# Down projection of layer 1 as seven Strassen products per pair of chunks, in two passes, on one Trainium2 core

## The chip, the cores and the metric

The kernel is one program on one core of a Trainium2 chip. The metric is the time of one execution on the device in microseconds, the median of three runs.

## The reference, cut to what matters

The model is an encoder of two layers over 1024 tokens of 1024 channels. Each layer ends in a SwiGLU feed-forward part of width 2816, and the last step is a norm:

```python
def swiglu_ffn(h, w_gate, w_up, w_down):
    return (jax.nn.silu(h @ w_gate) * (h @ w_up)) @ w_down
...
        h = rmsnorm(x, norm_ffn_g[layer])
        x = x + swiglu_ffn(h, ffn_w_gate[layer], ffn_w_up[layer], ffn_w_down[layer])
    return rmsnorm(x, final_g)
```

The change concerns the last product, `@ w_down`, for layer 1, what comes right before it (the activations silu(gate) * up) and right behind it (residual sum and final norm).

## The kernel before, in words

Everything lies transposed: channels on the 128 partitions, tokens along the free axis. The residual is 8 tiles `xs[k]` of 128 channels by 1024 tokens. The hidden width is 22 chunks of 128. All products are in fp32 accuracy from three matmuls of the shorter type fp32r: an operand is split into a high part (a cast on ACT, L87) and the rest (a subtraction on DVE, L88), and `mm3` (L98) adds high x high, high x low and low x high in one PSUM bank.

The program is recorded in Python order; a scheduler then sets the order on each engine and places the waits, and each engine goes through its own list in order. Buffers come from pools of a fixed number: 28 `big` tiles (one holds a 512-token operand with both of its parts, or one residual tile), 10 `w` tiles, 3 `raw` tiles for loads, 6 `half` tiles, and two each of `cv` and `pr`. An allocation waits until a tile of its pool is free.

Gate and up (`gate_up_first` L608, `gate_up_all` L684). The feed-forward part already takes its first two products as Strassen's seven in Winograd's form: two chunks of the hidden width, two halves of the channels and two halves of the tokens (`HALVES`, 512 each). `prep` (L626) forms the weight sums for a pair `p` (11 pairs) one unit of products ahead, `gate_up_rest` (L655) does the products, `fin` (L647) takes silu or the product with up and sends the activation to DRAM (`a_dram`) from GpSimd's queue (L653). GpSimd does nothing else in this stage.

Down (`down`, L737). The first half of the tokens comes whole, then the second. For each half the hidden chunks go in groups of 8, 7 and 7 (`GROUPS`). `load_a` (L708) loads the activations of a group back and splits them, `load_w` (L108) loads and splits the weights of a group for one of the 8 output chunks, and `down_one` (L721) accumulates the chunks of a group in one PSUM bank and adds the bank to the residual on DVE (L726). That is 22 x 8 x 3 matmuls of 512 columns for the first half and, because the second half is given in two parts of 256 tokens, twice as many of 256 columns for the second. `final` (L876) squares and sums the residual over the channels (L133, L134, a matmul with ones L538), takes the root (L122 to L125), scales (L882) and stores (L884). For the first half it runs behind the products of the second; `run_behind` (L728) hands out its instructions. For the last 256 tokens it is the tail of the program.

## Time and profile before

| what | value |
|---|---|
| the three runs | 1743.06, 1745.55 and 4281.53 us, median 1745.55 |
| span of the profiled execution | 1740.6 us, first to last instruction |
| matmuls, TensorE busy | 8318 in 1682.0 us |
| DVE, ACT, GpSimd (POOL) busy | 1245.9, 692.9, 276.0 us |
| granted TensorE clock | 0.991 on average |
| moved by DMA | 238.66 MB, 137 GB/s |

The third run is an outlier of the machine and takes no part in what follows. The time of a run holds some start and end around the span: the median lies 4.95 us over the span of the profiled execution, whose own time is not listed apart. A row of the profile gives the line of the code, the engine, the operation, output and inputs with their form, the count, then the busy time, the mean length of one and the idle time before it with what ended it. PEld is TensorE's loading of weights, which runs beside its matmuls; SP is the engine whose queue issues most loads.

### The profile page before, as it was taken

How to read it: one execution, taken by the hardware profiler on the slowest of the kernel's cores; microseconds unless marked ns; L12 is line 12 of the kernel's file. 1: busy time of each engine (PE TensorE's matmuls, PEld its weight loads, DVE VectorE, ACT ScalarE, POOL GpSimd, SP SyncE). 2: the span in 40 equal slices, each digit the busy share in tenths (PEclk: the TensorE clock that was granted, in tenths of full speed). 3: DMA queues.
4: the chain of work that ended last, by engine and by line, in shares of the span. 5: the costliest groups of instructions: out<-in, count | busy, mean ns of one | idle time of the engine just before them, and what ended most of it. 6: DMA issues, size and time to landing. Idle time of an engine off the chain costs nothing.

```text
span 1740.6 us, 22375 instructions
## 1 busy us (share of the span) xinstructions
PE 1682.0 (97%) x8318; PEld 1400.9 (80%) x8318; DVE 1245.9 (72%) x1774; ACT 692.9 (40%) x1062; POOL 276.0 (16%) x300
## 2 busy tenths in 40 slices
PE   6998899999999999999999998999999999999997
PEld 4786777777888888889998886778888888788997
DVE  8699988794577777755559768787777775545546
ACT  5455855464323232233234344553232322334223
POOL 4587764111000000000000001110000000000000
PEclk9999899999999999999999999999999999999999
DMA  5121311545633333355433425646333333644433
GB/s 188 47 97 37 135 61 46 184 142 201 232 131 122 127 109 127 116 167 174 133 109 126 152 85 182 211 163 218 133 122 127 109 127 121 204 144 160 167 122 123
DMA packets 82236, 238.66 MB, mean 137 GB/s; under 512 B 10320, under 2 KB 15696, under 8 KB 82128
## 3 DMA queue, kind: packets, MB, share of 16 engines
q1 hardware_dynamic: 65520, 186.64, 32.6%
q0 software_dynamic: 14304, 47.46, 7.2%
q10 hardware_dynamic: 2304, 3.15, 0.5%
q8 instruction: 65, 1.06, 0.3%
q14 instruction: 43, 0.35, 0.1%
HBM read 190.02 MB, written 47.19 MB: 136 GB/s over the span
## 4 chain that ended last, share of the span: by engine, by line
PE 83%; DVE 11%; DMA 3%; ACT 1%; issue 1%; SPq 0%; DVEq 0%; ACTq 0%
PE ps L100 18%; PE ps L102 18%; PE ps L101 18%; PE lnp L100 10%; PE lnp L102 10%; PE lnp L101 9%; DVE acc L313 2%; DVE acc L134 1%; DMA xin<-in_xT 1%; DMA raw<-in_wd 1%; DVE hl L88 1%; DMA raw<-in_wu 1%; DVE wl L88 1%; DVE ybl L88 0%; PE lnp L538 0%
## 5 line engine op out<-in xcount | busy, mean ns | idle before, releaser
L87 ACT CAST hl<-raw 128x512 fp32r<-128x512 f32 x264 | 161.2, 621 | 426.0 <-DVE raw L636 161.4
L100 PE MATMUL ps<-hl 128*128 128x512 f32 x704 | 277.6, 395 | 3.3 <-ACT s L617 2.8
L102 PE MATMUL ps<-hl 128*128 128x512 f32 x704 | 276.6, 393 | 0.0
L101 PE MATMUL ps<-hl 128*128 128x512 f32 x704 | 276.5, 393 | 0.0
L87 ACT CAST wh<-raw 128x896 fp32r<-128x896 f32 (+2 forms) x139 | 132.5, 953 | 243.5 <-PE ps L101 109.0
L100 PE MATMUL ps<-ahl,wh 128*128 128x256 f32 (+3 forms) x711 | 228.0, 321 | 0.5 <-ACT wh L87 0.5
L102 PE MATMUL ps<-ahl,wl 128*128 128x256 f32 (+3 forms) x711 | 227.7, 320 | 0.5 <-DVE wl L88 0.5
L101 PE MATMUL ps<-ahl,wh 128*128 128x256 f32 (+3 forms) x711 | 227.2, 320 | 0.0
L88 DVE TENSOR_TENSOR hl<-raw,hl 128x512 fp32r<-128x512 f32 x264 | 179.8, 689 | 47.9 <-ACT hl L87 43.3
L100 PE MATMUL lnp<-hl 128*128 128x512 f32 x528 | 210.2, 398 | 0.7 <-ACT s L617 0.7
L102 PE MATMUL lnp<-hl 128*128 128x512 f32 x528 | 208.1, 395 | 0.0
L101 PE MATMUL lnp<-hl 128*128 128x512 f32 x528 | 207.9, 394 | 0.0
L88 DVE TENSOR_TENSOR wl<-raw,wh 128x896 fp32r<-128x896 f32 (+2 forms) x127 | 141.6, 1116 | 48.7 <-ACT wh L87 44.3
L100 PEld LDWEIGHTS ps<-hl 128*128 128x128 f32 x704 | 132.2, 188 | 37.7 <-ACT s L617 6.9
L102 PEld LDWEIGHTS ps<-hl 128*128 128x128 f32 x704 | 132.3, 188 | 30.6
L101 PEld LDWEIGHTS ps<-hl 128*128 128x128 f32 x704 | 132.4, 188 | 29.6
L303 POOL TENSOR_TENSOR cvp<-cvp,pr 128x512 f32<-128x512 f32 x96 | 139.3, 1452 | 82.5 <-ACT pr L302 78.2
L100 PEld LDWEIGHTS ps<-ahl,wh 128*128 128x128 f32 x711 | 134.3, 189 | 11.1 <-ACT wh L87 0.9
L102 PEld LDWEIGHTS ps<-ahl,wl 128*128 128x128 f32 x711 | 134.0, 189 | 10.9 <-DVE wl L88 1.0
L101 PEld LDWEIGHTS ps<-ahl,wh 128*128 128x128 f32 x711 | 134.3, 189 | 10.2 <-issue 0.2
L653 POOL DMA_DIRECT2D a<-g x66 | 35.6, 540 | 576.6 <-DVE g L652 576.6
L100 PEld LDWEIGHTS lnp<-hl 128*128 128x128 f32 x528 | 99.5, 189 | 27.3 <-ACT s L617 4.3
(209 smaller groups left out, 3095.9 us busy)
## 6 DMA issues: line engine op xcount, KB each, us to landing
raw<-in_wg SPq DMA_DIRECT2D x66, 512.0 KB, 3.4
raw<-in_wu SPq DMA_DIRECT2D x66, 512.0 KB, 3.6
raw<-in_wd SPq DMA_DIRECT2D x72, 448.0 KB, 3.3
a<-g POOLq DMA_DIRECT2D x88, 256.0 KB, 3.1
raw<-in_wd SPq DMA_DIRECT2D x32, 512.0 KB, 3.8
p<-s POOLq DMA_DIRECT2D x44, 256.0 KB, 3.2
u<-p SPq DMA_DIRECT2D x44, 256.0 KB, 4.2
raw<-a SPq DMA_DIRECT2D x44, 256.0 KB, 3.3
```

The costliest lines, as they stand in the source:

```text
L87: nc.scalar.copy(hi, src)
L88: (eng or nc.vector).tensor_tensor(out=lo, in0=src, in1=hi.bitcast(F32), op=ALU.subtract)
L100: nc.tensor.matmul(ps, lh, rh, start=start, stop=False, **kw)
L101: nc.tensor.matmul(ps, lh, rl, start=False, stop=False, **kw)
L102: mm = nc.tensor.matmul(ps, ll, rh, start=False, stop=stop, **kw)
L134: TT(out=acc, in0=acc, in1=sq, op=ALU.add)
L303: nc.gpsimd.tensor_tensor(out=a, in0=a, in1=pr, op=ALU.add)
L313: STT(out=acc, in0=src, scalar=wv, in1=acc, op0=ALU.mult, op1=ALU.add)
L653: nc.gpsimd.dma_start(a_dram[layer][m][:, HALVES[t]], dst)
```

## The change

The down projection of layer 1 becomes `down_strassen`. Layer 0 keeps `down`. The left operand A is the weight matrix for a pair of hidden chunks by a pair of output chunks (A11, A12 for the first output chunk, A21, A22 for the second; `j` counts the 4 pairs of output chunks), the right operand B the activations of the pair of hidden chunks by the two halves of the tokens. The seven products in Winograd's form are A11 B11, A12 B21, S1 T1, S2 T2, S3 T3, S4 B22 and A22 T4, with S1 = A21 + A22, S2 = S1 - A11, S3 = A11 - A21, S4 = A12 - S2 and T1 = B12 - B11, T2 = B22 - T1, T3 = B22 - B12, T4 = B21 - T2.

The sums T1 to T4 are made on GpSimd at the end of each pair of the gate and up stage (`combine`) and go to DRAM in place of B12, together with B11, B21 and B22. The sums of weights are made on DVE (`left_a`, `left_b`) from the raw weights, which come in a new layout `wds` and are loaded twice. Pass A takes five of the products, in blocks of 3, 3, 3 and 2 pairs, for each block 4 steps `j`; pass B takes S1 T1 and S4 B22 in blocks of 4, 4 and 3. A finished bank is copied to SBUF by ACT and added to the residual (or to the partial sum `u2`) by GpSimd (`add_pool`), except S2 T2, S4 B22 and, in the last block of pass A, A22 T4, which DVE adds from PSUM. Right operands of the next block are loaded and split during the block before. The final norm takes each half of the tokens whole, the second one as the tail.

```diff
+    PTT = nc.gpsimd.tensor_tensor
...
     def fin(layer, up, dst, src, m, t, tmp=None):
...
-            nc.gpsimd.dma_start(a_dram[layer][m][:, HALVES[t]], dst)
+            store_b(layer, "B%d%d" % (m % 2 + 1, t + 1), m // 2, dst)
+
+    def store_b(layer, name, p, src):
+        if layer == 0:
...
+        elif name != "B12":
+            nc.gpsimd.dma_start(b_dram[name][p], src)
+
+    def combine(p, g):
+        g11 = arena.tile([P, TH], F32, tag="cv", name="g11", bufs=2)
+        nc.sync.dma_start(g11, b_dram["B11"][p])
+        t1, t3 = g11, arena.tile([P, TH], F32, tag="cv", name="t3", bufs=2)
+        t2, t4 = (arena.tile([P, TH], F32, tag="pr", name=n, bufs=2) for n in ("t2", "t4"))
+        PTT(out=t3, in0=g["22"], in1=g["12"], op=ALU.subtract)
+        PTT(out=t1, in0=g["12"], in1=g11, op=ALU.subtract)
+        PTT(out=t2, in0=g["22"], in1=t1, op=ALU.subtract)
+        PTT(out=t4, in0=g["21"], in1=t2, op=ALU.subtract)
+        for name, src in (("T1", t1), ("T2", t2), ("T3", t3), ("T4", t4)):
+            store_b(1, name, p, src)
...
+            if up and layer == 1:
+                combine(p, g)
...
+    def load_b(names, early=False):
+        out = []
+        for n, p in names:
+            if early:
+                raw = half("rawb")
+            else:
+                bturn[0] += 1
+                tag = ("cv", "pr")[bturn[0] % 2]
+                raw = arena.tile([P, TH], F32, tag=tag, name=tag, bufs=2)
+            nc.sync.dma_start(raw, b_dram[n][p])
+            out.append(opnd(raw, big))
+        return out
...
+    def load_quads(j, p0, n):
+        out = []
+        for q in range(2):
+            raw = arena.tile([P, 1024], F32, tag="raw", name="raw", bufs=3)
+            rv = raw.rearrange("p (a c) -> p a c", a=2)[:, :, :n * P]
+            nc.sync.dma_start(rv, wds[j, :, 2 * q:2 * q + 2, p0 * P:(p0 + n) * P])
+            out += [raw[:, :n * P], raw[:, TH:TH + n * P]]
+        return out
...
+    def left_a(j, p0, n):
+        a11, a12, a21, a22 = load_quads(j, p0, n)
+        w = {"A11": wopnd(a11)}
+        s3 = small("s3")[:, :n * P]
+        TT(out=s3, in0=a11, in1=a21, op=ALU.subtract)
+        TT(out=a21, in0=a21, in1=a22, op=ALU.add)
+        TT(out=a21, in0=a21, in1=a11, op=ALU.subtract)
+        w["S2"], w["S3"], w["A12"], w["A22"] = wopnd(a21), wopnd(s3), wopnd(a12), wopnd(a22)
+        return w
+
+    def left_b(j, p0, n):
+        a11, a12, a21, a22 = load_quads(j, p0, n)
+        TT(out=a21, in0=a21, in1=a22, op=ALU.add)
+        TT(out=a11, in0=a21, in1=a11, op=ALU.subtract)
+        TT(out=a12, in0=a12, in1=a11, op=ALU.subtract)
+        return {"S1": wopnd(a21), "S4": wopnd(a12)}
+
+    def down_strassen(layer, blocks_a, blocks_b, gen):
...
+        def add_pool(dst, ps):
+            t = half("u1")
+            nc.scalar.copy(t, ps)
+            PTT(out=dst, in0=dst, in1=t, op=ALU.add)
+
+        def finish_b(bc, s4, b22, x12):
+            product(bc, s4, b22, False, True)
+            TT(out=x12, in0=bc, in1=x12, op=ALU.add)
+
+        for i, (kind, p0, n, j) in enumerate(steps):
...
+            nw = left(i + 1) if i + 1 < len(steps) else None
+            (x11, x12), (x21, x22) = x[j]
+            if kind == "a":
+                ba, bb, bd = single(), single(), single()
+                product(ba, w["A11"], b["B11"], True, True)
+                if u2[j] is None:
+                    u2[j] = arena.tile([P, TH], F32, tag="cvp", name="uu", bufs=4)
+                    nc.scalar.copy(u2[j], ba)
+                else:
+                    add_pool(u2[j], ba)
+                product(bb, w["S2"], b["T2"], True, True)
+                TT(out=u2[j], in0=bb, in1=u2[j], op=ALU.add)
+                product(bd, w["S3"], b["T3"], True, True)
+                add_pool(x22, bd)
+                product(ba, w["A12"], b["B21"], False, True)
+                add_pool(x11, ba)
+                product(bd, w["A22"], b["T4"], False, True)
+                if (p0, n) != blocks_a[-1]:
+                    add_pool(x21, bd)
+                else:
+                    TT(out=x21, in0=bd, in1=x21, op=ALU.add)
+                    TT(out=x21, in0=x21, in1=u2[j], op=ALU.add)
+                    for dst in (x12, x22):
+                        PTT(out=dst, in0=dst, in1=u2[j], op=ALU.add)
+            else:
+                bc = single()
+                product(bc, w["S1"], b["T1"], True, True)
+                add_pool(x22, bc)
+                if late:
+                    finish_b(*late)
+                late = bc, w["S4"], b["B22"], x12
...
+            got += load_b(todo[:k])
...
-    down(1, ([(0, TH)], [(TH, TH + 256), (TH + 256, S)]), final)
+    down_strassen(1, ((0, 3), (3, 3), (6, 3), (9, 2)), ((0, 4), (4, 4), (8, 3)), final)
```

Three places show how the engines' lists change. In the rows below `g` are the activations of a pair, `hl` a split operand (`hl<-raw` a left one, `hl<-rawb`, `hl<-pr` and `hl<-cv` right ones), `uu` the partial sum `u2`, `ps` and `lnp` PSUM banks. Line numbers of the new kernel are those of its own file: there L89 is the subtraction of a split, L664 a store, L672 to L675 `combine`, L883 the add of `add_pool`.

On GpSimd, the end of its list before, from the last pair of the gate and up stage on:

```order
L653 DMA a_18_2345<-g_11518 128x512
L653 DMA a_21_2348<-g_11718 128x512
L653 DMA a_21_2348<-g_11719 128x512
L653 DMA a_20_2347<-g_11720 128x512
L972 UNCONDITIONAL_BRANCH
```

and the same pair now, with the first adds of the down projection:

```order
L664 DMA bB_10_2359<-g_11893 128x512
L664 DMA bB_10_2348<-g_11894 128x512
L672 TENSOR_TENSOR t_12048<-g_11893,g_11895 128x512
L673 TENSOR_TENSOR g_12046<-g_11895,g_12046 128x512
L664 DMA bT_10_2392<-t_12048 128x512
L674 TENSOR_TENSOR t_12049<-g_11893,g_12046 128x512
L664 DMA bT_10_2370<-g_12046 128x512
L675 TENSOR_TENSOR t_12050<-g_11894,t_12049 128x512
L664 DMA bT_10_2381<-t_12049 128x512
L664 DMA bT_10_2403<-t_12050 128x512
L883 TENSOR_TENSOR x_12157<-x_12157,u_12241 128x512
L883 TENSOR_TENSOR x_12159<-x_12159,u_12229 128x512
```

Where GpSimd had nothing left, four sums of the last pair stand now, and 76 adds follow them.

On DVE, the transition: the last unit of the gate and up stage before, in which the splits of the first activations (`ahl`) stand between its sums,

```order
L88 TENSOR_TENSOR ahl<-raw,ahl 128x512 x2
L670 TENSOR_TENSOR u_11824<-lnp,u_11824 128x512
L652 TENSOR_TENSOR g_11718<-u_11824,g_11718 128x512
L88 TENSOR_TENSOR ahl<-raw,ahl 128x512 x2
L677 TENSOR_TENSOR c_11853<-lnp,u_11797 128x512
L652 TENSOR_TENSOR g_11719<-c_11853,g_11719 128x512
L88 TENSOR_TENSOR wl<-raw,wh 128x1024
L681 TENSOR_TENSOR u_11797<-lnp,u_11797 128x512
L652 TENSOR_TENSOR g_11720<-u_11797,g_11720 128x512
```

and now, from the same product of the same unit on:

```order
L694 TENSOR_TENSOR u_11999<-lnp,u_11999 128x512
L89 TENSOR_TENSOR hl<-s_12180,hl 128x384
L656 TENSOR_TENSOR g_11893<-u_11999,g_11893 128x512
L701 TENSOR_TENSOR c_12028<-lnp,u_11972 128x512
L89 TENSOR_TENSOR hl<-raw,hl 128x384
L656 TENSOR_TENSOR g_11894<-c_12028,g_11894 128x512
L705 TENSOR_TENSOR u_11972<-lnp,u_11972 128x512
L89 TENSOR_TENSOR hl<-rawb,hl 128x512
L656 TENSOR_TENSOR g_11895<-u_11972,g_11895 128x512
L89 TENSOR_TENSOR hl<-rawb,hl 128x512 x4
L89 TENSOR_TENSOR hl<-raw,hl 128x384
L89 TENSOR_TENSOR hl<-rawb,hl 128x512 x2
```

The splits between the sums are those of left operands now, and the right operands of the first block come behind the sum L705, which reads the last product of the stage.

On DVE, well inside the down projection: before, one step of the first half of the tokens and the next,

```order
L726 TENSOR_TENSOR x_11880<-ps,x_11880 128x512
L88 TENSOR_TENSOR wl<-raw,wh 128x896
L88 TENSOR_TENSOR ahl<-raw,ahl 128x512
L726 TENSOR_TENSOR x_11882<-lnp,x_11882 128x512
L88 TENSOR_TENSOR wl<-raw,wh 128x896
L88 TENSOR_TENSOR ahl<-raw,ahl 128x512
```

and now, one step in the fourth block of pass A:

```order
L903 TENSOR_TENSOR uu<-ps,uu 128x512
L836 TENSOR_TENSOR s_13544<-raw 128x256
L837 TENSOR_TENSOR raw<-raw 128x256
L838 TENSOR_TENSOR raw<-raw 128x256
L89 TENSOR_TENSOR hl<-raw,hl 128x256
L89 TENSOR_TENSOR hl<-s_13544,hl 128x256
L89 TENSOR_TENSOR hl<-raw,hl 128x256
L912 TENSOR_TENSOR x_12163<-lnp,x_12163 128x512
L89 TENSOR_TENSOR hl<-raw,hl 128x256
L913 TENSOR_TENSOR x_12163<-x_12163,uu 128x512
```

Three instructions for a step of 21 matmuls have become ten for one of 30, and the splits of left operands are five small ones (one stands ahead of these rows) in place of one long one.

More of the change, by code (lines that the diff above doesn't have):

```diff
@@ L43, in trunk @@
 def trunk(ctx: ExitStack, tc: tile.TileContext, xT, vecs, cw, w_in, w_out, fmap, pmap,
-          wg, wu, wd, cen_m, pcnt, dft_h, dft_l, seq_h, seq_l, out):
+          wg, wu, wd, wds, cen_m, pcnt, dft_h, dft_l, seq_h, seq_l, out):
     nc = tc.nc
@@ L527, in single @@
         return bank(("ps", "lnp", "ps")[turn[0] % 3])
-    a_dram = [[dram.tile([P, S], F32, name=f"a{layer}_{f}") for f in range(NF)] for layer in range(2)]
+    a_dram = [[dram.tile([P, S], F32, name=f"a0_{f}") for f in range(NF)]]
+    b_dram = {n: [dram.tile([P, TH], F32, name=f"b{n}_{p}") for p in range(NF // 2)]
+              for n in ("B11", "B21", "B22", "T1", "T2", "T3", "T4")}
     def norm(lo, hi):
@@ L548, in product @@
     def product(ps, w, b, start, stop):
-        for j in range(4):
+        n = len(b)
+        for j in range(n):
             c = j * P
             mm3(ps, (w[:, c:c + P], w[:, TH + c:TH + c + P]), (b[j][:, :TH], b[j][:, TH:]),
-                start and j == 0, stop and j == 3, skip_group_check=not start)
+                start and j == 0, stop and j == n - 1, skip_group_check=not start)
     def h_make(layer, t, bt, hf):
@@ L623, in gate_up_first @@
                 TT(out=g, in0=ps, in1=g, op=ALU.mult)
-        nc.gpsimd.dma_start(a_dram[layer][2 * p][:, HALVES[0]], g)
+        store_b(layer, "B11", p, g)
     def prep(layer, p, wsrc, first):
@@ L770, in down @@
         run_behind(back, 1e9)
+    def load_b(names, early=False):
[10 more added lines that the diff above has]
+        return out
+    bturn = [0]
+    def load_quads(j, p0, n):
[6 more added lines that the diff above has]
+        return out
@@ new lines, in wopnd @@
+    def wopnd(src):
+        t = wtile("hl")
+        n = src.shape[-1]
+        split(t[:, :n], t[:, TH:TH + n], src)
+        return t
+    PASS_A = (("A11", "B11"), ("S2", "T2"), ("S3", "T3"), ("A12", "B21"), ("A22", "T4"))
+    def left_a(j, p0, n):
[7 more added lines that the diff above has]
+        return w
@@ L874, in trunk, with final @@
     gate_up_all(1, b1, NP1)
-    def final(pi, blocks):
-        for lo, hi in blocks:
-            inv = norm(lo, hi)
-            yield 6.0
-            for k in range(KD):
-                o = half("o")[:, :hi - lo]
-                STT(out=o, in0=xs[k][:, lo:hi], scalar=gneg[:, V_FIN + k:V_FIN + k + 1], in1=inv,
-                    op0=ALU.mult, op1=ALU.mult)
-                (nc.sync if k % 2 else nc.scalar).dma_start(out[k][:, lo:hi], o)
-                yield 0.65
-    down(1, ([(0, TH)], [(TH, TH + 256), (TH + 256, S)]), final)
+    def final(t):
+        hs = HALVES[t]
+        inv = norm(hs.start, hs.stop)
+        yield 6.0
+        for k in range(KD):
+            o = half("o")
+            STT(out=o, in0=xs[k][:, hs], scalar=gneg[:, V_FIN + k:V_FIN + k + 1], in1=inv,
+                op0=ALU.mult, op1=ALU.mult)
+            (nc.sync if k % 2 else nc.scalar).dma_start(out[k][:, hs], o)
+            yield 0.65
+    down_strassen(1, ((0, 3), (3, 3), (6, 3), (9, 2)), ((0, 4), (4, 4), (8, 3)), final)
 def _round_f32r(a):
@@ L947 @@
     wd = []
-    for l in range(2):
+    for l in range(1):
         parts, o = [], 0
@@ L954 @@
     a["wd"] = np.stack(wd)
+    a["wds"] = np.ascontiguousarray(
+        f["ffn_w_down"][1].reshape(NF // 2, 2, P, 4, 2, P).transpose(3, 2, 4, 1, 0, 5)).reshape(4, P, 4, NF // 2 * P)
     a["cen"] = (np.eye(P) - 1.0 / P).astype(np.float32)
```

39 lines of the change are left out of this document (added).

## The prediction

> **What bounds the kernel now.** I read the page first, then the stages in windows, then the timeline at both ends of the stage that changes. The page gives TensorE nearly the whole span, and its chain of waits says the same:
>
> ```profile
> PE 1682.0 (97%) x8318; PEld 1400.9 (80%) x8318; DVE 1245.9 (72%) x1774; ACT 692.9 (40%) x1062; POOL 276.0 (16%) x300
> PE 83%; DVE 11%; DMA 3%; ACT 1%; issue 1%; SPq 0%; DVEq 0%; ACTq 0%
> ```
>
> The windows cut the end of the program into four: the gate and up products of layer 1, the two halves of the tokens in its down projection, and the tail (length, then busy time and count of PE, PEld, DVE, ACT and POOL, granted clock, DMA share, GB/s).
>
> ```profile
> 1162.00:1479.80 317.80, 317.01 (x1373) 256.93 (x1371) 231.12 (x356) 96.53 (x159) 19.43 (x36) 1.00 0.40 140
> 1479.80:1602.00 122.20, 121.67 (x526) 98.77 (x527) 68.67 (x85) 45.79 (x60) 0.54 (x1) 1.00 0.52 169
> 1602.00:1729.80 127.80, 127.70 (x1063) 126.62 (x1062) 73.45 (x123) 40.76 (x57) 0.00 (x0) 1.00 0.44 143
> 1729.80:1740.60 10.80, 0.70 (x2) 0.30 (x2) 5.51 (x13) 0.89 (x2) 0.00 (x0) 0.73 0.29 97
> ```
>
> In the down projection TensorE does not pause, DVE is busy for 57%, and GpSimd does nothing: this stage costs what its matmuls cost. Its first matmul, the first of the second half and the last are
>
> ```profile
> 1479.78 0.50 PE L100 MATMUL ps<-ahl,wh 128*128 128x512 f32 x1 [0.51 <-ACT wh L87]
> 1602.52 0.28 PE L100 MATMUL ps<-ahl,wh 128*128 128x256 f32 x1
> 1729.47 0.28 PE L102 MATMUL lnp<-ahl,wl 128*128 128x256 f32 x1
> ```
>
> The first half is 22 x 8 x 3 = 528 matmuls of 512 columns in 122.74 us, so one takes 0.2325 us when they follow each other (the 0.39 us that the groups give for one is its passage, which overlaps the next). The second half is twice as many of 256 columns, 0.1205 us each. Together 250.0 us, to 1729.75.
>
> **The change, part by part.**
>
> *Removed: matmuls.* Seven products instead of eight, 11 pairs of chunks, 4 pairs of output chunks, three matmuls each: 924 of 512 columns, 924 x 0.2325 = 214.8 us. That is 35.2 us less, 2.0% of the span, and it is all that the change can win. Pass A holds three blocks of 180 matmuls (41.9 us each) and one of 120 (27.9 us), pass B 264 (61.4 us).
>
> *Added on DVE.* What one instruction takes stands in these groups, and the distance of two that follow each other in the timeline rows under them:
>
> ```profile
> L88 DVE TENSOR_TENSOR hl<-raw,hl 128x512 fp32r<-128x512 f32 x264 | 179.8, 689 | 47.9 <-ACT hl L87 43.3
> L88 DVE TENSOR_TENSOR wl<-raw,wh 128x896 fp32r<-128x896 f32 x72 | 78.5, 1090 | 16.6 <-ACT wh L87 15.4
> 1473.36 0.69 DVE L88 TENSOR_TENSOR ahl<-raw,ahl 128x512 fp32r<-128x512 f32 x1 [0.64 <-ACT ahl L87]
> 1473.97 0.68 DVE L670 TENSOR_TENSOR u<-lnp,u 128x512 f32<-128x512 f32 x1
> 1441.63 0.68 DVE L636 TENSOR_TENSOR raw<-raw 128x512 f32<-128x512 f32 x1
> 1442.35 0.69 DVE L643 TENSOR_TENSOR raw<-raw 128x512 f32<-128x512 f32 x1
> ```
>
> 512 columns take 0.61 us in a row, 0.72 where the second needs the first; (1090 - 689) / 384 = 1.04 ns a column makes 0.48 us of 384 columns and 0.34 us of 256. I counted the DVE instructions of the new order by place. Between the transition and the last product there are 289: 25.1 us of work in the first block of pass A, 29.4 in the second, 24.2 in the third, 23.1 in the fourth (its steps are short, but it also makes the right operands of pass B), 53.3 in pass B with the final norm of the first token half. Dependent pairs add about 0.65 us a step, 2.6 a block. Alone, that is 155 + 13 us against 214.8 of TensorE: DVE would be hidden, closest to the bound in pass B.
>
> *Added on GpSimd.* 76 adds of 512 columns in the down projection (12, 16, 16 and 20 in the blocks of pass A, 12 in pass B), and 4 for each of 11 pairs in the gate and up stage. What they do to DVE shows early in the trace, where both run without pause, and where DVE runs on alone:
>
> ```profile
> 17.30:30.30 13.00, 8.59 (x23) 5.43 (x23) 13.00 (x10) 5.09 (x9) 12.22 (x8) 1.00 0.42 142
> L162 DVE SCALAR_TENSOR_TENSOR gxl<-xin,gneg,gxh 128x512 fp32r<-128x512 f32 x6 | 9.9, 1682 | 0.0
> L162 DVE SCALAR_TENSOR_TENSOR gxl<-xin,gneg,gxh 128x512 fp32r<-128x512 f32 x7 | 4.7, 740 | 0.0
> 130.56 1.51 DVE L434 TENSOR_TENSOR at<-at 128x256 f32<-128x256 f32 x1
> 133.41 0.41 DVE L436 TENSOR_TENSOR at<-zs 128x256 f32<-128x256 f32 x1
> L303 POOL TENSOR_TENSOR cvp<-cvp,pr 128x512 f32<-128x512 f32 x96 | 139.3, 1452 | 82.5 <-ACT pr L302 78.2
> L461 DVE TENSOR_TENSOR wcl<-ps,wch 128x512 fp32r<-128x512 f32 x16 | 10.9, 682 | 0.7 <-ACT wch L460 0.7
> ```
>
> The second row is from the 12.5 us in which GpSimd adds, the third from the 4.6 us behind them: the same instruction takes 1.68 us beside an add and 0.74 alone. They take turns, one DVE instruction to each of 8 GpSimd ones in 13.0 us, 1.62 us a pair; DVE alone needs 4.7 / 7 = 0.67. So an add takes 0.95 us from DVE. The row at 130.56 gives 1.51 - 0.41 = 1.10; an add that falls into a pause of DVE, or beside an instruction that reads PSUM (the last row: 682 ns, in the stretch where GpSimd adds too), costs nothing. I take 0.95, since DVE is nearly full, with 0 and 1.10 for the range.
>
> The Trainium skill ("SBUF — State Buffer", Who interferes with whom) says that a DVE instruction with two SBUF inputs contends with a GpSimd instruction that reads SBUF, and that whichever starts first holds the shared ports for its whole length. The trace agrees in kind (1.68 us against 0.74, and 0.68 with a PSUM input); by the letter of the rule an add would cost its full length, which is a rival below.
>
> *Added on ACT.* The casts are as many as the splits; the copies out of PSUM are new to this stage.
>
> ```profile
> L87 ACT CAST hl<-raw 128x512 fp32r<-128x512 f32 x264 | 161.2, 621 | 426.0 <-DVE raw L636 161.4 <-PE lnp L102 123.6 <-PE ps L102 101.2
> L617 ACT COPY s<-ps 128x512 f32<-128x512 f32 x22 | 12.9, 584 | 8.6 <-PE ps L102 7.6 <-ACT hl L87 1.1
> ```
>
> A step of pass A has 5 casts of 384 columns (0.5 us), on average 3.75 of 512 and up to 4 copies: 7.2 us of the 10.5 of TensorE. A copy that comes late holds the product which accumulates on the same bank (A12 B21 after A11 B11); two products, 4.2 us, lie between, so I cost it at nothing. Were the casts of four right operands in front of the copy and nothing between, it would be 2.5 us in each of 12 steps, 30 us.
>
> *By place*, with adds at 0.95: first block 25.1 + 2.6 + 11.4 = 39.1 us (TensorE 41.9 bounds), second 29.4 + 2.6 + 15.2 = 47.2 (DVE), third 42.0 (even), fourth 23.1 + 1.8 + 19.0 = 43.9 (TensorE has 27.9: DVE bounds by 16), pass B 53.3 + 4 + 11.4 = 68.7 (TensorE 61.4: DVE by 7). The larger of each: 41.9 + 47.2 + 42.0 + 43.9 + 68.7 = 243.7.
>
> *Moved: the transition.* Before, the activations of the first down stage are split between the last gate and up sums, and TensorE waits 0.51 us. Now all 15 right splits but the first stand behind the last of these sums on DVE: 11.3 us of DVE work, and the 4 adds of the last pair with 3.8. TensorE can use it up to the end, 15.1 + 0.7 us, having 10.5 + 2.1 us of products to do meanwhile: +3.2.
>
> *Loads.* Each step loads two quarters of weights into 3 raw buffers, and one can only be issued when an earlier split has freed its buffer.
>
> ```profile
> raw<-in_wd SPq DMA_DIRECT2D x72, 448.0 KB, 3.3
> ```
>
> Behind those 3.3 us DVE has right splits and PSUM sums to do in most steps. I allow 0.15 us for each of 28 steps, 4 us. In bytes the stage grows from 122.2 x 169 + 127.8 x 143 GB/s = 39 MB to 23 of weights (twice), 20 of right operands and 8 of residual and output, 52 MB in some 250 us or 205 GB/s; at 169 the queues were busy for 0.52, so this is 0.63: no bound.
>
> *Tail.* The two quarter-width ends become one of 512 columns:
>
> ```profile
> 1729.79 0.42 DVE L726 TENSOR_TENSOR x<-lnp,x 128x256 f32<-128x256 f32 x1 [1.14 <-PE lnp L102]
> 1731.24 0.70 PE L538 MATMUL lnp<-acc,onesd 128*128 128x256 f32 x2 [1.48 <-DVE acc L134]
> 1736.34 1.33 DVE L882 SCALAR_TENSOR_TENSOR o<-x,gneg,v 128x256 f32<-128x256 f32 x3 [0.36 <-DMA out<-o]
> L538 PE MATMUL lnp<-acc,onesd 128*128 128x512 f32 x2 | 1.0, 592 | 0.0
> L882 DVE SCALAR_TENSOR_TENSOR o<-x,gneg,v 128x512 f32<-128x512 f32 x8 | 5.5, 745 | 0.0
> L134 DVE TENSOR_TENSOR acc<-acc,sq 128x512 f32<-128x512 f32 x7 | 4.8, 686 | 0.1
> ```
>
> 10.85 us now. Then: the sum and its square 0.5 more, four accumulations in place of one 2.3, the matmul 0.3, the three steps of the root and its start 1.0, eight outputs 5.5 for 3.8, the store 0.1: +5.9.
>
> *Gate and up.* 44 adds take 42 us from DVE, which is busy for 231 of 317.8 us; its left operands are made a unit of products ahead. Cost 0; without that cover, half of it, 21 us.
>
> **The sum.** 250.0 becomes 3.2 + 243.7 + 4 = 250.9, +0.9; tail +5.9; with 1 us for what the gate and up stage lets through, +7.8 on a span of 1740.6. That span lies 5.0 under the median of the runs, 1745.55; carried over, 1753, or 0.4% more. The 35 us that TensorE saves go to DVE, mostly in the fourth block and in pass B. A measurement of this kernel can tell about 2% (35 us) from no change.
>
> **The rivals.**
>
> *The adds hide* (0.16). If they fall on pauses and PSUM reads, TensorE bounds all blocks: 3.2 + 214.8 + 4, tail 5.9, so 1745.55 - 22 = 1723. For it: 32 of 289 DVE instructions read PSUM. Against it: the 13 us above, in which no add was hidden. Even so it is no 2%.
>
> *The loads come onto the path* (0.13): slower. The step's second quarter waits for a buffer, lands 3.3 us later, and four or five DVE instructions of the step wait in order behind it, and TensorE for them. Half of the 3.3 us exposed in each of 28 steps is 46 us, of which 4 are in the sum: 1795. It decides from 1.1 us a step (1780). For it: in pass B a step has only 5.6 us of TensorE, and the chain of one load and three sums fills it. Against it: the right splits are ordered between.
>
> *An add costs its whole length* (0.10): 1.45 us, as in its row, instead of 0.95, on 48 adds of the blocks where DVE bounds: +24, 1777. This is the rule of the skill's page by the letter. Against it: 1.62 us for a pair is less than the two lengths.
>
> *The gate and up stage gives way* (0.08): half of the 42 us reaches TensorE, 1774.
>
> **Chances and range.** Forecast 0.53, at 1753, its own range 1738 to 1768. Faster by 2% (under 1710) needs more than all the hidden adds: 0.03. Slower by 2% (over 1780): most of the loads' case and the edges of the last two, 0.14. The rest, 0.83, within. The range 1722 to 1785 leaves out the loads' worst and little else.
>
> **What would show it.** Right: the last matmul near 250 us after the first of the down projection; DVE over 90% busy in the fourth block and pass B; L89 splits at 1.1 us and more beside L883 adds; TensorE's idle time ended by DVE; TensorE unbroken in the first block and in the gate and up stage. Wrong: TensorE over 95% busy all through (adds hide), or idle ended by DMA into raw (loads), or gaps before 1479 (gate and up).

## The result

The changed kernel took 1814.72 us (median; 1810.76 to 1815.45), the kernel before it on the same chip 1744.30: a ratio of 1.0404, 95% interval 1.0388 to 1.042. It is slower by 70 us, where 8 were predicted, and outside the range of 1722 to 1785.

The page of the changed kernel has the same two rows as before at its head (busy time of the engines; the chain that ended last, by engine):

```profile
PE 1676.7 (92%) x7656; PEld 1356.5 (75%) x7656; DVE 1381.8 (76%) x1885; ACT 737.2 (41%) x1206; POOL 470.3 (26%) x453
PE 62%; DVE 18%; DMA 8%; issue 7%; ACT 2%; POOL 2%; SPq 0%; DVEq 0%; ACTq 0%; POOLq 0%
```

TensorE has 662 matmuls fewer (in the down stage 528 of 512 columns and 1056 of 256 became 924 of 512), but now fills 92% of the span instead of 97%, and its share of the chain fell from 83% to 62%. The windows show where. They are cut at the gate and up stage, at the first matmul of each block of the down stage (180, 180, 180, 120 and 264 matmuls), and at the tail (length, busy time and count of PE, PEld, DVE, ACT, POOL, granted clock, DMA share, GB/s):

```profile
1164.00:1509.20 345.20, 322.06 (x1374) 258.47 (x1372) 266.56 (x362) 94.75 (x160) 89.63 (x106) 0.99 0.44 147
1509.20:1569.00 59.80, 47.88 (x182) 35.88 (x180) 42.02 (x58) 30.64 (x60) 21.62 (x19) 0.91 0.72 245
1569.00:1618.90 49.90, 42.73 (x181) 33.52 (x180) 43.59 (x56) 25.60 (x53) 25.95 (x17) 1.00 0.51 151
1618.90:1668.00 49.10, 44.44 (x182) 35.52 (x181) 40.28 (x53) 24.89 (x52) 22.86 (x16) 0.93 0.43 130
1668.00:1709.20 41.20, 30.88 (x122) 23.14 (x121) 38.66 (x46) 17.47 (x38) 27.25 (x18) 0.96 0.47 139
1709.20:1796.30 87.10, 70.03 (x267) 51.36 (x265) 73.08 (x100) 33.36 (x59) 26.84 (x16) 0.92 0.50 155
1796.30:1813.70 17.40, 1.32 (x2) 0.30 (x2) 11.17 (x17) 2.11 (x4) 0.00 (x0) 0.64 0.32 121
```

The span grew by 73.1 us, from 1740.6 to 1813.7: 2.0 had gathered before layer 1's gate and up stage begins; that stage takes 27.4 more (its end moved from 1479.8 to 1509.2); the down stage 37.1 more (287.1 for 250.0); the tail 6.6 more (17.4 for 10.85). The stage whose cost was put at 0 gives the second largest part.

**The gate and up stage.** In nine places TensorE stands for 2.5 to 2.7 us (from the start of one matmul to the next, less the usual 0.23), and in a tenth, behind a late cast, for 1.7. One of the nine in the timeline (start, length, engine, line, operation; in brackets the idle time before it and what ended it), first GpSimd's `combine`, then DVE, then TensorE:

```profile
1451.78 1.28 POOL L672 TENSOR_TENSOR t<-g,g 128x512 f32<-128x512 f32 x1 [2.04 <-DVE g L656]
1453.03 1.74 POOL L673 TENSOR_TENSOR g<-g,g 128x512 f32<-128x512 f32 x1
1455.30 1.30 POOL L674 TENSOR_TENSOR t<-g,g 128x512 f32<-128x512 f32 x1
1457.12 1.30 POOL L675 TENSOR_TENSOR t<-g,t 128x512 f32<-128x512 f32 x1
...
1451.95 1.66 DVE L638 TENSOR_TENSOR s<-raw 128x512 f32<-128x512 f32 x1 [0.26 <-DMA raw<-in_wg]
1453.65 1.67 DVE L639 TENSOR_TENSOR raw<-raw 128x512 f32<-128x512 f32 x1
1455.84 1.32 DVE L640 TENSOR_TENSOR raw<-raw 128x512 f32<-128x512 f32 x1
1457.19 1.78 DVE L647 TENSOR_TENSOR raw<-raw 128x512 f32<-128x512 f32 x1
1459.50 0.68 DVE L692 TENSOR_TENSOR g<-ps,u 128x512 f32<-128x512 f32 x1
...
1457.57 0.40 PE L103 MATMUL ps<-hl 128*128 128x512 f32 x1
1460.32 0.47 PE L101 MATMUL ps<-hl 128*128 128x512 f32 x1 [2.36 <-DVE g L692]
```

Four weight sums that take 0.69 us before take 1.3 to 1.8 beside GpSimd's four. Behind them in DVE's order stands L692, which adds bank bd (S3 T3) into `u3`; and A22 T4, the product at 1460.32, accumulates on that same bank, with only S1 T1 (2.76 us) between. So TensorE does not wait for its left operands, which are indeed a unit ahead, but for a bank to be emptied. The waits count it for the whole stage (what waited, for what: us, times, longest); they are measured from the end of the matmul before, and besides the nine hold one of 0.3:

```profile
PE ps L101 <- DVE g L692: 21.7, 10, 2.6
```

**The down stage.** Here half of the 51 us in which TensorE stands (287.1 - 235.96) end with a copy by ACT out of a bank, 16.3 + 8.8 us, and the copies stand behind casts. From the second half of the first block (ACT, then TensorE, then GpSimd):

```profile
1562.41 0.62 ACT L88 CAST hl<-cv 128x512 fp32r<-128x512 f32 x1 [2.81 <-DMA cv<-bB]
...
1566.63 0.57 ACT L882 COPY u<-lnp 128x512 f32<-128x512 f32 x1
...
1563.96 0.39 PE L102 MATMUL ps<-hl 128*128 128x512 f32 x1
1567.26 0.50 PE L101 MATMUL lnp<-hl 128*128 128x512 f32 x1 [2.91 <-ACT u L882]
...
1567.28 1.57 POOL L883 TENSOR_TENSOR x<-x,u 128x512 f32<-128x512 f32 x1 [8.14 <-ACT u L882]
```

The product in bank lnp had been complete since 1561.8 (its last matmul starts at 1561.42), and TensorE's next product accumulates on that bank. ACT got to it at 1566.6, since a cast in front had waited 2.81 us for its load and six more stood behind that one. In this place it was a load that held the casts; over the stage they wait longer for DVE's weight sums (69.4 us) than for loads (32.3 us). GpSimd, the engine that was to take work off DVE, waited 8 us for the same copy. Over the down stage:

```profile
POOL x L883 <- ACT u L882: 126.6, 35, 15.1
ACT hl L88 <- DVE raw L838: 32.0, 10, 9.4
PE lnp L101 <- ACT u L882: 16.3, 7, 4.7
PE ps L101 <- ACT u L882: 8.8, 5, 5.3
```

By the place of the matmuls in their step, all of the row with lnp are A22 T4 (bank bd, with one product between its two, A12 B21), all of that with ps A12 B21 (bank ba, with two). No wait of ACT ends with an instruction of GpSimd, so the copies did not lack a buffer that an add still held.

### The profile page after: what moved, and what is told of

Read it like the earlier page. It is cut to its first block, busy times and chain, and to the rows that moved or that the text cites. A ratio compares the mean times of both kernels' runs of the same rounds, so it can differ in the third digit from the quotient of the medians.

```text
span 1813.7 us, 21653 instructions
## 1 busy us (share of the span) xinstructions
PE 1676.7 (92%) x7656; PEld 1356.5 (75%) x7656; DVE 1381.8 (76%) x1885; ACT 737.2 (41%) x1206; POOL 470.3 (26%) x453
## 4 chain that ended last, share of the span: by engine, by line
PE 62%; DVE 18%; DMA 8%; issue 7%; ACT 2%; POOL 2%; SPq 0%; DVEq 0%; ACTq 0%; POOLq 0%
PE ps L101 13%; PE ps L102 13%; PE ps L103 13%; PE lnp L101 7%; PE lnp L103 7%; PE lnp L102 7%; DVE hl L89 4%; DMA raw<-in_wds 3%; DVE acc L314 2%; DVE acc L135 1%; DMA bT<-g 1%; DMA xin<-in_xT 1%; POOL t L674 1%; DMA raw<-in_wu 1%; DVE o L1048 1%
## 5 line engine op out<-in xcount | busy, mean ns | idle before, releaser
L88 ACT CAST hl<-raw 128x512 fp32r<-128x512 f32 (+2 forms) x352 | 205.5, 594 | 530.1 <-DVE raw L640 184.7
L101 PE MATMUL ps<-hl 128*128 128x512 f32 x896 | 358.1, 401 | 42.8 <-DVE g L692 21.9
L102 PE MATMUL ps<-hl 128*128 128x512 f32 x896 | 356.1, 398 | 4.5 <-DVE hl L89 4.5
L103 PE MATMUL ps<-hl 128*128 128x512 f32 x896 | 355.6, 397 | 3.5 <-DVE hl L89 3.5
L89 DVE TENSOR_TENSOR hl<-raw,hl 128x512 fp32r<-128x512 f32 (+2 forms) x352 | 251.8, 723 | 58.7 <-ACT hl L88 54.7
L101 PE MATMUL lnp<-hl 128*128 128x512 f32 x644 | 260.3, 404 | 18.3 <-ACT u L882 16.3
L103 PE MATMUL lnp<-hl 128*128 128x512 f32 x644 | 255.7, 397 | 0.8 <-DVE hl L89 0.8
L102 PE MATMUL lnp<-hl 128*128 128x512 f32 x644 | 255.7, 397 | 0.0
L101 PEld LDWEIGHTS ps<-hl 128*128 128x128 f32 x896 | 170.2, 190 | 94.6 <-issue 26.1
L102 PEld LDWEIGHTS ps<-hl 128*128 128x128 f32 x896 | 170.7, 191 | 45.1 <-DVE hl L89 7.7
L103 PEld LDWEIGHTS ps<-hl 128*128 128x128 f32 x896 | 170.3, 190 | 44.5 <-DVE hl L89 5.4
L101 PEld LDWEIGHTS lnp<-hl 128*128 128x128 f32 x644 | 122.7, 191 | 54.6 <-ACT u L882 19.6
L103 PEld LDWEIGHTS lnp<-hl 128*128 128x128 f32 x644 | 122.7, 191 | 30.5 <-DVE hl L89 2.0
L102 PEld LDWEIGHTS lnp<-hl 128*128 128x128 f32 x644 | 123.0, 191 | 28.4 <-issue 1.2
L88 ACT CAST wh<-raw 128x1024 fp32r<-128x1024 f32 (+2 forms) x83 | 78.0, 939 | 116.0 <-PE ps L102 37.7
L883 POOL TENSOR_TENSOR x<-x,u 128x512 f32<-128x512 f32 x56 | 87.1, 1562 | 137.5 <-ACT u L882 126.6
L101 PE MATMUL ps<-ahl,wh 128*128 128x504 f32 (+2 forms) x358 | 115.2, 322 | 0.0
L103 PE MATMUL ps<-ahl,wl 128*128 128x504 f32 (+2 forms) x358 | 114.8, 321 | 0.0
L102 PE MATMUL ps<-ahl,wh 128*128 128x504 f32 (+2 forms) x358 | 114.7, 320 | 0.0
L89 DVE TENSOR_TENSOR wl<-raw,wh 128x896 fp32r<-128x896 f32 (+2 forms) x71 | 78.1, 1102 | 29.9 <-ACT wh L88 26.2
```

Source lines behind the costliest of these rows:

```text
L88: nc.scalar.copy(hi, src)
L89: (eng or nc.vector).tensor_tensor(out=lo, in0=src, in1=hi.bitcast(F32), op=ALU.subtract)
L101: nc.tensor.matmul(ps, lh, rh, start=start, stop=False, **kw)
L102: nc.tensor.matmul(ps, lh, rl, start=False, stop=False, **kw)
L103: mm = nc.tensor.matmul(ps, ll, rh, start=False, stop=stop, **kw)
L883: PTT(out=dst, in0=dst, in1=t, op=ALU.add)
```

## The experiments

Each ratio is to the kernel before on the same chip, with its 95% interval. Stretch is the time from the first to the last matmul of the down stage, 250.0 us before and 287.1 in the changed kernel; the matmuls alone take 214.8.

**Which of GpSimd's work costs what.** Theory: a GpSimd sum or add and a DVE instruction with two SBUF inputs take turns, and both stages pay for it. Rivals: the loads, or the copies and casts on ACT. The first run puts `combine` on DVE:

```
-        PTT(out=t3, in0=g["22"], in1=g["12"], op=ALU.subtract)
+        TT(out=t3, in0=g["22"], in1=g["12"], op=ALU.subtract)
...
```

> The four sums T1 to T4 of each pair in the gate and up stage are made by DVE instead of GpSimd; the down projection is untouched. Theory: a GpSimd sum keeps a DVE instruction with two SBUF inputs waiting, and the DVE sum that reads a bank (L692 in the new kernel) then comes 2.5 us too late for the product that accumulates on the same bank, 11 times. The 11 gaps vanish or shrink to under 1 us: 27 us less, some of it back because DVE now does 44 sums of 0.61 us itself; 1788 to 1797 against 1814.7. Rival: the pair is held by the load of B11 and the stores of T1 to T4, which the chain of waits names; these stay, so the gaps stay and the time is above 1808.

Measured: 1779.71 us, 1.0208 (1.0193 to 1.0223). The gaps of the gate and up stage are gone. One weight sum's group in the changed kernel, and then the stage's window and the same group in this one,

```profile
L639 DVE TENSOR_TENSOR raw<-raw 128x512 f32<-128x512 f32 x21 | 23.4, 1116 | 0.7
```

```profile
1162.00:1479.90 317.90, 317.30 (x1374) 257.40 (x1373) 256.10 (x403) 93.99 (x161) 35.72 (x66) 1.00 0.47 160
L639 DVE TENSOR_TENSOR raw<-raw 128x512 f32<-128x512 f32 x21 | 14.4, 688 | 0.4
```

show TensorE unbroken with DVE at 256 us, more than the 231 it has in the kernel before. In the changed kernel it had 266.56. 40 of the 44 sums lie in this window: on GpSimd they cost DVE 35.4 us, 0.89 each, and on DVE itself 25.0, 0.62 each (both differences also hold a few first instructions of the down stage). Some 10 us of DVE make 27 us of time: it is less the amount that matters than in front of what it falls.

The second run leaves `combine` on GpSimd and puts the down stage's adds on DVE, straight from the bank:

```
-            t = half("u1")
-            nc.scalar.copy(t, ps)
-            PTT(out=dst, in0=dst, in1=t, op=ALU.add)
+            TT(out=dst, in0=ps, in1=dst, op=ALU.add)
```

> The down projection adds every finished bank on DVE straight from PSUM; no copy by ACT and no add by GpSimd there (the gate and up sums stay on GpSimd). Theory (turns between GpSimd and DVE): DVE gets 76 x 0.61 = 46 us of its own, 168 + 46 = 214 us in a stage of 214.8 us of matmuls, and loses the waits; the stage goes from 287 to 240 to 250 us, the time to 1768 to 1778. Rival (loads): the chain of 3 raw buffers stays as it is and DVE is as full as before, so the stage stays at 270 or more, 1798 or more.

1781.28 us, 1.0227 (1.0206 to 1.0248): the gate and up gaps stay, the stretch falls to 252. The third run does both:

> Both: GpSimd does no sum in the gate and up stage of layer 1 nor in the down projection. Theory: both gains add, 1741 to 1760, level with the kernel before. Rival (loads, stores): 1785 or more.

1746.98 us, 1.0027 (1.0018 to 1.0037), stretch 247.4. The two parts add up: 35.0 and 33.4 alone, 67.7 together. GpSimd's 120 instructions, with the 68 copies that feed some of them, are nearly the whole loss against the kernel before, all but 4 us. The loads are the same in this run, so they are not what cost the 70 us.

The fourth run is the changed kernel without the 76 additions themselves, which are left out (the eight of `u2` too, not shown here) while ACT's copies stay:

```
             t = half("u1")
             nc.scalar.copy(t, ps)
-            PTT(out=dst, in0=dst, in1=t, op=ALU.add)
```

> The down projection leaves out the 76 GpSimd adds (the ACT copies out of PSUM stay, and nothing uses them); the gate and up sums stay on GpSimd. The output lacks those terms. Theory: nothing keeps DVE waiting and it has no more to do than in the change, 168 us of 215; the stage goes from 287 to 230 to 240 us, the time to 1758 to 1768, under e2. Rival (loads): 275 us, 1802.

1778.07 us, 1.02 (1.0181 to 1.0219): the expected time was missed. With no add at all, but with the copies, the stage takes 248.0 us, only 4 less than in the second run, where all adds are on DVE and the copies are gone. A later run leaves out both additions and copies, on the kernel with everything on DVE:

```
         def add_pool(dst, ps):
-            TT(out=dst, in0=ps, in1=dst, op=ALU.add)
+            pass
```

> The kernel with all sums and adds on DVE (1747.0, stretch 247.4 us), with 68 of the down stage's adds left out together with the eviction of their banks; the eight additions of u2 to x12 and x22 stay. Leaves out part of the computation: the products in those banks reach no output. If DVE's time is what holds the stretch (68 adds of 0.6 us, 41 us of DVE): the stretch falls to 222 to 232 and the time to 1722 to 1732. If it is the loads and the weight sums with their casts, as the run without adds but with copies (stretch 248) suggests: 240 to 247, 1740 to 1747.

1739.15 us, 0.9982 (0.9972 to 0.9991), stretch 238.1. The down stage in one row each: the changed kernel, the fourth run, all on DVE, neither adds nor copies.

```profile
1509.20:1796.30 287.10, 235.96 (x927) 179.41 (x925) 237.63 (x308) 131.95 (x259) 124.52 (x84) 0.94 0.53 166
```

```profile
1513.76:1761.75 247.99, 225.23 (x927) 174.09 (x925) 178.69 (x308) 132.59 (x259) 7.99 (x9) 0.98 0.61 193
```

```profile
1479.60:1727.10 247.50, 228.02 (x927) 175.45 (x925) 220.12 (x391) 99.23 (x191) 2.16 (x4) 0.97 0.60 193
```

```profile
1481.50:1719.60 238.10, 223.73 (x927) 173.95 (x925) 179.56 (x322) 98.10 (x191) 2.16 (x4) 0.99 0.63 201
```

The first two have the same 308 DVE instructions and the same copies; with the adds on GpSimd DVE takes 58.9 us longer, 0.78 us an add on average, and the stage 39.1. Without the adds ACT's casts wait 41.2 us for DVE's weight sums instead of 69.4, and TensorE's waits for copies fall from 25.1 us to this row of the fourth run:

```profile
PE lnp L101 <- ACT u L882: 3.6, 6, 0.9
```

So the way from the adds to TensorE is DVE's sums, the casts behind them, and the copies behind the casts; these waits are 21.5 of the 39.1 us. In the last two, 68 adds on DVE are 40.6 us of DVE and 9.3 of the stage. The second stretch is 9.9 us above the last; some 4 of that belong to the first block and to the sums of `combine` still on GpSimd there (55.5 us in the second run, 51.4 in the third), which leaves about 6 for 68 copies, though ACT has only 132 us of work in 248 (each stretch is that of one execution, so this is rough). Even without adds and copies the stage is 23 us above its matmuls.

**Is the place where DVE is the bound the only one that pays?** On the first run's kernel, the adds of the fourth block and of pass B go to DVE, those of the first three blocks stay on GpSimd:

```
+            if kind == "b" or (p0, n) == blocks_a[-1]:
+                TT(out=dst, in0=ps, in1=dst, op=ALU.add)
+                return
             t = half("u1")
```

> The layer's T sums on DVE (as in the run that gave 1779.7), and of the down stage's adds those of the first three blocks of pass A stay copied by ACT and added by GpSimd; those of the fourth block and of pass B are done by DVE straight from the bank. If GpSimd's adds cost time only where DVE is the bound (fourth block and pass B, as the prediction's sum has it): 1746 to 1753. If they cost everywhere, by lengthening the weight sums for which ACT's casts and behind them its copies wait: 32 us spread over 76 adds, 44 of them kept, gives 1760 to 1770.

1762.83 us, 1.0117 (1.0097 to 1.0136): within the second expectation. The 44 adds of the first three blocks cost 15.9 us against all on DVE (0.36 each), the other 32 cost 16.9 (0.53 each). So adds also cost outside the fourth block and pass B, but not evenly: the first block took 51.8 us (51.4 with all on DVE), the second 52.6 (42.0), the third 44.9 (42.3). The expectation left out that the prediction's sum has DVE as the bound of the second block too, at 47.2; that block took 5.4 more than this, with DVE busy for 44.7 of its 52.6 us.

**Is the tie in the gate and up stage the bank?** The first try wrote the next unit's weight sums behind the additions of bb and bd.

> The changed kernel with its GpSimd sums and adds kept; in layer 1's gate and up only the place of the next unit's weight sums is moved: for every gate unit behind an up unit they stand on DVE behind the additions of the banks bb and bd (u2 and u3) instead of ahead of them. Theory (the tie is the bank: TensorE's product A22 T4 has to accumulate on bank bd, and the addition that empties it stands in DVE's order behind four weight sums that the GpSimd sums lengthen): the 2.5 us gap in front of A22 T4 goes, gate-and-up idle falls from 27 us to under 10, the time to 1788 to 1798. Rival (the left operands come late): the sums are now later still, the gap moves to the start of the next unit and grows, 1815 to 1840.

1814.05 us, 1.0402 (1.0384 to 1.042). It tells nothing: the scheduler put the sums back in front, and DVE's order of sums and additions came out as it was. With a dependency it held:

```
-        TT(out=u3, in0=bd, in1=u2, op=ALU.add)
+        add = TT(out=u3, in0=bd, in1=u2, op=ALU.add)
+        nxt = mid(add)
...
+            tc.add_manual_dep(ins.ins, after.ins.name, ...)
```

> The edit of the run before that moved the weight sums, now with a dependency that holds them: in the changed kernel, in every gate unit behind an up unit, the first weight sum of the next unit depends on the addition of bank bd into u3, so that on DVE both additions (u2 and u3) stand ahead of the four sums that collide with GpSimd's. GpSimd's sums and adds stay. Theory (the tie is bank bd, needed again by A22 T4): the 2.5 us gaps go, gate-and-up idle falls from 27 us to under 10, 1788 to 1798. Rival (the left operands come late): the gap moves to the next unit's first product, 1812 to 1840.

1807.44 us, 1.0366 (1.0348 to 1.0383): 7 us gained, where the theory asked for 17 to 27. DVE and TensorE in this kernel (L695 is the addition of bd here, L692 that of bb):

```profile
1448.69 0.69 DVE L695 TENSOR_TENSOR g<-ps,u 128x512 f32<-128x512 f32 x1 [2.12 <-PE ps L103]
1449.42 1.06 DVE L638 TENSOR_TENSOR s<-raw 128x512 f32<-128x512 f32 x1
...
1464.11 0.69 DVE L692 TENSOR_TENSOR u<-ps,u 128x512 f32<-128x512 f32 x1 [0.28 <-DMA u<-p]
1465.92 1.89 DVE L89 TENSOR_TENSOR hl<-raw,hl 128x512 fp32r<-128x512 f32 x3
1467.73 0.68 DVE L695 TENSOR_TENSOR u<-lnp,u 128x512 f32<-128x512 f32 x1
...
1468.46 0.50 PE L101 MATMUL lnp<-hl 128*128 128x512 f32 x1 [2.27 <-DVE u L695]
```

In the gate unit the addition now comes as soon as its product is done, and the gap there is gone. But the weight sums run later, the loads behind them too, and in the next unit the addition of bd stands behind five splits: the same tie, one unit on. The waits of this stage:

```profile
PE lnp L101 <- DVE u L695: 16.3, 10, 2.3
```

Late left operands would have stopped TensorE at a unit's first product, and no such wait of length arose. The tie is the bank, with 2.76 us of room; which DVE work stands in front of it depends on the order.

**What keeps the stage at 247 us with nothing on GpSimd.** All on the kernel of the third run. First, loads that may run ahead in pass B, from the ten buffers of the `w` pool instead of three (`spare` is set in pass B alone):

```
-            raw = arena.tile([P, 1024], F32, tag="raw", name="raw", bufs=3)
+            raw = (arena.tile([P, 1024], F32, tag="w", name="rawq", bufs=10) if spare else
+                   arena.tile([P, 1024], F32, tag="raw", name="raw", bufs=3))
```

> The kernel with all sums and adds on DVE (1747.0), and in pass B the weight quadrants are loaded into tiles of the ten-buffer w pool instead of the three raw tiles, so the loads may start steps ahead. If the idle time of pass B (gaps at 1640, 1647, 1681, 1713, 1718, 1723, some 11 us) comes from loads that wait for a raw tile: 1738 to 1743. If it comes from DVE, which has 93% of those 48 us, or from the right operands' loads: 1745 to 1748.

1754.81 us, 1.0066 (1.0044 to 1.0089): worse than either expectation. In pass B TensorE now waits more for evictions (1.5 us of this row in the third run),

```profile
PE ps L101 <- DVE x L882: 6.3, 6, 1.5
```

With other buffers the scheduler also ordered DVE otherwise in pass B, so this run does not tell the loads alone; all it shows is that the free buffers, with that order, gave nothing. Then the queues, in two ways: right operands and x on GpSimd's queue, and x alone there, two loads a step, each pair behind the last product of the step before:

```
-            nc.sync.dma_start(raw, b_dram[n][p])
+            (nc.sync if early else nc.gpsimd).dma_start(raw, b_dram[n][p])
```

> The kernel with all sums and adds on DVE (1747.0), with the loads of x and of the right operands behind the first block's issued on GpSimd's queue, so that the weight quadrants alone stand on SyncE's. If the gaps at 1480 to 1492 and 1515 to 1525 (3.4 and 3.6 us, and 2 us of matmuls at 425 ns behind the second) come from quadrants that stand behind other loads in SyncE's order: 1739 to 1743. If the transfers themselves are the limit there (DMA share 0.95 from 1480 to 1500): 1745 to 1749.

> The kernel with all sums and adds on DVE (1747.0, stretch 247.4), with the eight loads of x (512 KB each) on GpSimd's queue, two for each step of the first block, each pair behind the last product of the step before. If the gaps between 1480 and 1525 (7 us, 2 more at half pace) come from quadrants and right operands that stand behind 4 MB of x: 1739 to 1744. If the sum of the bytes is the limit there: 1745 to 1749.

1756.75 us, 1.0075 (1.005 to 1.0099), and 1751.77, 1.0044 (1.0028 to 1.0059): both slower than either of their expectations. The gaps do not shrink: the first block takes 53.9 us with right operands and x on the other queue and 55.0 with x in turn, 51.4 in the third run, and in the first of the two the second block grows as well, from 42.0 to 49.8. In the third run and in that with x in turn the first 20 us of the stage are

```profile
1480.00:1500.00 20.00, 17.63 (x69) 12.59 (x70) 17.45 (x30) 10.93 (x21) 2.16 (x4) 1.00 0.95 344
```

```profile
1480.00:1500.00 20.00, 14.07 (x50) 9.84 (x49) 12.76 (x22) 9.04 (x17) 4.42 (x9) 0.88 0.96 343
```

with the DMA engines busy for 0.95 and 0.96 at the same 344 and 343 GB/s in either order: this points to the bytes as the limit there, though no run moved fewer of them. Next, the block of two pairs first instead of last, alone and with x in turn:

```
-    down_strassen(1, ((0, 3), (3, 3), (6, 3), (9, 2)), ((0, 4), (4, 4), (8, 3)), final)
+    down_strassen(1, ((0, 2), (2, 3), (5, 3), (8, 3)), ((0, 4), (4, 4), (8, 3)), final)
```

> The kernel with all sums and adds on DVE (1747.0, stretch 247.4), with the block of two hidden pairs in pass A as the first instead of the last. If DVE's time is the bound at the step from pass A to pass B (DVE unbroken from 1633 to 1653 while TensorE stands 5 us and runs 3 us at half pace), a block of three there gives each step 21 instead of 14 us for the same adds: these 5 to 8 us go, 1738 to 1743, unless the first block now lacks them (its products are done sooner than x and the next right operands are loaded): then 1745 to 1752.

> Both edits of the two runs before: if each takes its share away, 1733 to 1740, which would be faster than the kernel before (1743); if they meet in the first block, 1743 to 1750.

1748.53 us, 1.0024 (1.0015 to 1.0034), and 1751.01, 1.0034 (1.0019 to 1.0049). Alone, pass B is 4.0 us shorter (78.3 for 82.3) and the step to it has no gap, but the first block meets the transfers with less work in hand (43.1 us for 27.9 of matmuls, with pauses of 4.3 and 4.6). Neither gain came; the first run lies where its expectation has the first block as the limit, the second 1 us above its own. Last, the first token half's norm moved behind the last product:

```
-                    back, budget = [gen(0)], 0.0
...
+        for _ in gen(0):
+            pass
```

> The kernel with all sums and adds on DVE (1747.0), with the first token half's norm and output taken out of pass B and put behind the last product. If TensorE's norm matmul, which waits in order for DVE's sum of squares, and the norm's share of DVE are what pass B lacks: the stretch from first to last down matmul falls from 247.4 to 240 to 243 and the tail grows by 8 to 12, 1749 to 1755. If pass B is held by its loads: the stretch stays at 245 to 248, 1754 to 1760.

1752.23 us, 1.0043 (1.0029 to 1.0057). Pass B falls from 82.3 to 73.7 us and the tail grows by 11.6. Its rows, the third run's first:

```profile
1644.70:1727.00 82.30, 70.07 (x267) 51.48 (x265) 73.65 (x123) 25.96 (x44) 0.00 (x0) 0.94 0.59 184
```

```profile
1644.20:1717.90 73.70, 66.90 (x267) 49.08 (x265) 64.12 (x107) 22.91 (x38) 0.00 (x0) 0.98 0.58 177
```

9.5 us of DVE left the pass, and 8.6 us of time with it. That fits DVE as the bound of pass B, but does not show it: TensorE's wait for the norm's sum of squares (2.5 us) left with it, and in the run with neither adds nor copies pass B has 12.7 us less of DVE than in the third and is only 6.5 us shorter:

```profile
1643.80:1719.60 75.80, 68.94 (x267) 50.60 (x265) 60.90 (x102) 23.10 (x40) 0.00 (x0) 0.95 0.62 187
```

No version beat the kernel before by anything that counts.

## Why the prediction was wrong

By its own terms, in us. The blocks' columns are the trace's distances between the first matmuls of the blocks; the first has the transition in it.

| term | predicted | changed kernel | all on DVE | neither adds nor copies |
|---|---|---|---|---|
| gate and up, more than before | 0 (1 allowed) | 27.4 | 0 | 0 |
| first block, transition | 45.1 | 59.8 | 51.4 | 51.3 |
| second block | 47.2 | 49.9 | 42.0 | 41.7 |
| third block | 42.0 | 49.0 | 42.3 | 41.6 |
| fourth block | 43.9 | 41.2 | 29.4 | 27.7 |
| pass B | 68.7 | 87.1 | 82.3 | 75.8 |
| loads | 4 | in the above | | |
| down stage | 250.9 | 287.1 | 247.4 | 238.1 |
| tail | 16.8 | 17.4 | 16.9 | 16.9 |

*The step that failed first* is "Gate and up. 44 adds take 42 us from DVE, which is busy for 231 of 317.8 us; its left operands are made a unit of products ahead. Cost 0". The 42 us were near (35.4 for the 40 sums in the stage). The cover was the wrong one: the left operands do have a unit of room, but DVE also empties the banks, in the same order, and one bank has 2.76 us. The rows that would have told stood in the trace of before. Both of these additions empty bank bd. L677, behind its second product, waited 28.2 us for 22 products; L668, between the two products, waited for only two of its 22, 4.2 us: in the others DVE came to it when its product was already done,

```profile
L668 DVE TENSOR_TENSOR g<-ps,u 128x512 f32<-128x512 f32 x22 | 15.1, 684 | 4.2 <-PE ps L102 4.1
L677 DVE TENSOR_TENSOR g<-ps,u 128x512 f32<-128x512 f32 x22 | 15.2, 691 | 28.2 <-PE ps L102 28.2
```

and one product later TensorE needs the bank. The rival priced this stage at 21 us and had 0.08; it came at 27.4. The runs with `combine` on DVE and with the forced order show it.

*The second* is "The larger of each: 41.9 + 47.2 + 42.0 + 43.9 + 68.7 = 243.7". DVE's amount came out right as a sum, but by luck, since two errors cancel: 168 of its own and 72 for the adds, 240; measured 178.7 without adds and 58.9 more with them, 237.6. The price of an add was too high, if anything (0.95; measured 0.78). But a block does not take the larger of two busy times. In the changed kernel's down stage DVE is busy for 83% of 287.1 us and TensorE for 82%: neither bounds it. TensorE waits for DVE through ACT and the banks, and what it loses so in one step it does not get back in the next, having only a product or two of room. The third block, called even, took 49.0.

*The third* is the copy: "two products, 4.2 us, lie between, so I cost it at nothing". Late copies ended 25.1 us of TensorE's waits in the changed kernel. Only 8.8 of them are at A12 B21, the product that the prediction looked at. The other 16.3 are at A22 T4: bank bd is copied too, behind S3 T3, and there only one product, 2.1 us, lies between. Where GpSimd added nothing, 68 copies still cost about 6 us.

*The fourth*, the transition and the loads (3.2 and 4), was too small in the first block: 51.3 us with no add and no copy, 9.4 above its matmuls; in its first 20 us the DMA engines were busy for 0.95 (third run). The bytes had been averaged over 250 us (0.63); those of the first 20 us were not looked at. The loads' rival did not hold: with the same loads and nothing on GpSimd the kernel takes 1746.98 us.

*Right* were the matmuls saved (with nothing on GpSimd the second and third blocks take 42 us, as the 0.2325 us had it), the tail (+6.6 for +5.9), and the fourth block in size (41.2 for 43.9, with DVE busy for 94%), though TensorE's waits there end with copies. DVE as the bound of pass B is right at most in part: DVE was busy for 84% of it in the changed kernel, where the prediction names over 90% as its sign, and its amount was short (73.1 us, and 73.65 with the adds on DVE, for 68.7).

What stays open: how the 23 us that the stage without adds and copies lies above its matmuls divide. Some 9 are in the first block and 14 in pass B, where the norm has a share; they were not taken apart further. The adds on GpSimd take some 15 us more of DVE than the same adds on DVE (58.9 against 43.5, the second run's 222.2 less the fourth's 178.7), and the stage is 35 us longer with them (287.1 against 252). How this comes about is shown for the waits behind copies; the rest of the 35 us, half-pace matmuls among it, was not summed up. Why the second block loses most with GpSimd's adds stays open too.

## What to carry to other kernels

Before work goes to an idle GpSimd, look at what the DVE instructions beside it stand in front of, above all evictions of a bank that a product needs again soon; here the time of the stage followed the shortest such room and not the sum of busy times. For each new wait, list every reader behind it in order on its engine, casts and copies included, and find the one with the least room. A stage in which several engines are over 80% busy is costed by following one step instruction by instruction, and its first 20 us of transfers by themselves.
